# Attention scores of two heads side by side in the rows of the matrix engine, with three split products, in a decoder layer's kernel

## The chip, the cores and the metric

The kernel runs on one core of one Trainium2 chip. Its time is the device time of one execution, in microseconds (us). The median of three runs of the kernel before is 627.21 us (626.58 to 627.97). One further execution was taken by the hardware profiler; all rows of the profile are from it.

## The reference

A decoder layer on x of 512 tokens by 1024 channels in float32, cut here to what bears on the change:

```python
proj = h @ w_in[l]
q, k, v, p, g = jnp.split(proj, [512, 1024, 1536, 2048], axis=-1)
y_attn = moba_attention(q, k, v, rel_bias) @ w_branch_attn      # 8 heads x 64
y_pool = multiscale_pool(p, w_pool_group, pool_scale) @ w_branch_pool
gates  = sigmoid(g)                                             # two of 1024 channels
mixed  = gates[:, :, 0] * y_attn + gates[:, :, 1] * y_pool
h = layer_norm(ALPHA * h + mixed @ w_out, ln1_g, ln1_b)
a, u = jnp.split(h @ w_ffn_in, 2, axis=-1)
f = (gelu(causal_dwconv(a)) * u) @ w_ffn_out
h = layer_norm(ALPHA * h + f, ln2_g, ln2_b)
```

With 512 tokens and blocks of 256 the block-sparse attention picks every earlier block, so each head is causal softmax attention: the scores are q·k/8 plus a bias that depends on the distance and on the head.

## The kernel before, in words

**Precision.** Matrix products are made of float32 values split into a high part (fp32r) and what is left, the low part: `split` (L74-79) writes the high part with ScalarE (ACT, L76) and the low part with VectorE (DVE, L77). A product of two split operands then takes three matmuls of TensorE (PE): `mm3` (L245-251) gives high x high, low x high and high x low. Weights are fetched by DMA as raw float32 and split on the chip (`wraw`, `araw` to `whi`, `wlo`).

**Stages.** The v columns of the input projection come first, then the pool columns, then `seven(("i", n))` for n = 0 to 4: a projection of 256 columns of weights by seven quarter products in place of eight. n = 0 gives two groups of the pool branch; n = 1 to 4 give q and k of the pairs of heads 0 to 3 (pair p has the heads 2p and 2p+1, each with 64 channels). In rows of the trace the seven products have the names `sai`, `sbi`, `sci`; their sums go into `quad` tiles, half q and half k. The attention follows, and with it the matmuls of the two branches (`br`), so that PE has other work beside the softmax. Then come the gates, the output projection, the first layer norm, the feed-forward part and the second layer norm, which the change does not touch.

**Channels lie on partitions.** q and k of a pair are tiles of 128 partitions: the even head in 0 to 63, the odd one in 64 to 127. PE contracts over partitions.

**head(h)** (L442-459) prepares one head for its scores. Q1 gets the high part of q/8 in the head's own 64 partitions (ACT, L455) and the low part in the other 64 (DVE, L456). K1 gets the high part of -k in its own half (ACT, L452), KL the low part (DVE, L453). Two DMAs from SBUF to SBUF on SyncE's queue (SP, L459) copy those halves of K1 and KL into the other 64 partitions. `*behind` names instructions which these four wait for in the order of issue.

**scores(h)** (L545-573). For each block of 128 queries two matmuls over all 128 partitions: Q1 with K1, Q1 with KL. As both halves of K1 hold the same, these are (q high + q low) x k high and (q high + q low) x k low: four split products. They have 256, 256, 384 and 512 columns (only keys up to the block). DVE adds the bias strip and takes the row's maximum (L560), negates it (L563); ACT takes exp with that as its bias and sums it (L566); DVE inverts the sums (L568); GpSimd (POOL) multiplies (L571). Tiles `pp`, `nm`, `rs` are from the pool `aw`, with three buffers each. Bias strips are loaded two heads ahead, with three buffers.

**trans(h)** (L615-634) transposes P on PE by ten matmuls of 128 columns with the identity, and copies the result from PSUM to `PT`. **pv(p)** (L636-646) multiplies P with v for both heads of a pair; its matmuls fill 64 columns of the array each, the even head in the first 64 and the odd one in the others.

**The order around the change.** Each engine works through its own row of instructions in order. A scheduler in the build puts the instructions of the program into these rows; it may move an instruction ahead of others that wait, but `tc.keep_in_program_order(ins)` pins one, and `tc.issue_after(ins)` puts what stands inside it behind `ins`. PSUM has eight banks, dealt out in turn by `bank`. In the projection's loop (L576-606), `head(0)` stands behind n = 2, `head(1)` and `scores(0)` behind n = 3. Behind n = 4 come `scores(1)`, and the loop over the heads (L671-704): `head(h + 2)` behind the maximum and exps of head h; a gate's projection or a branch matmul; `scores(h + 2)`; for even h the PV of the pair before; `trans(h)`. At h = 5 four loads of x and two loads of gate weights (`fetch_raw`, into gX and gD) are issued behind the last use of `state["dup"]`, the copies between partitions.

## Time and profile before

| what | value |
|---|---|
| median of three runs | 627.21 us (626.58 to 627.97) |
| the profiled execution | 628.95 us |
| its span in the profile | 627.3 us |
| its granted clock of TensorE, mean | 0.998 |
| 70 to 90 us (end of the projection, first scores) | busy: PE 20.00, DVE 16.07, ACT 15.51 |
| 90 to 109.2 us (gates' first projections, scores of heads 2, 3) | busy: PE 19.20, DVE 15.71, ACT 12.68 |
| 109.2 to 154 us (scores 4 to 7, PV, transposes, branches) | busy: PE 44.60 of 44.80, DVE 33.11, ACT 25.86 |

How to read it: the span is the time from the first to the last recorded instruction of the profiled execution; the execution's own time is 1.65 us longer. Busy times are by engine: PE (TensorE's matmuls), PEld (its weight loads, which overlap them), DVE, ACT, POOL, SP. Matmuls are pipelined, so the ends of neighbours overlap; how long one keeps PE is read from start to start. `L556` is line 556 of the kernel before. In a row of the timeline, `x3` is a row of three alike, and `[0.48 <-DVE nm L563]` says that the engine stood idle for 0.48 us, and which instruction ended that. A clock of 1.00 is TensorE's full rate.

### The profile page before, as it was taken

The page shows a single profiled execution, that of the slowest core. Times are in us where ns is not written, and L with a number is a line of the kernel's source. Part 1 is how long each engine was busy: PE and PEld are TensorE (multiplying, and loading weights), DVE is VectorE, ACT ScalarE, POOL GpSimd, SP SyncE. Part 2 cuts the span into 40 slices and gives each one's busy share as a digit, 9 for nine tenths or more (in the row PEclk, how much of TensorE's full clock was granted, in tenths as well). Part 3 has the DMA queues.
Part 4 walks back from the last instruction along what each step waited for, and adds up shares of the span by engine and source line. Part 5 has one row for each costly group of instructions (what it writes and reads, how often), then busy time and mean ns, then how long its engine had stood idle before and what let it go on. Part 6 is the DMA issues. An engine that isn't in the chain of part 4 may idle for free.

```text
span 627.3 us, 10677 instructions
## 1 busy us (share of the span) xinstructions
PE 615.9 (98%) x4096; PEld 555.9 (89%) x4096; DVE 519.1 (83%) x801; ACT 360.1 (57%) x549; POOL 123.6 (20%) x133
## 2 busy tenths in 40 slices
PE   8999999999999999999998999999999999999995
PEld 6899998876899998889998999999999888888884
DVE  6978887885978988399987988899888869788886
ACT  6636777673756567134665666565656356555452
POOL 0033134353512101110110111011000302123201
PEclk9999999999999999999999999999999999999999
DMA  8477644339687425807557886877744996889805
GB/s 321 144 201 197 168 120 133 102 102 303 182 202 189 99 71 166 321 14 243 127 151 187 216 188 167 201 187 205 195 105 139 336 262 132 202 194 205 208 1 134
DMA packets 42322, 110.08 MB, mean 175 GB/s; under 512 B 4496, under 2 KB 5016, under 8 KB 42016
## 3 DMA queue, kind: packets, MB, share of 16 engines
q1 hardware_dynamic: 28224, 72.82, 34.7%
q0 software_dynamic: 13472, 35.67, 30.0%
q10 hardware_dynamic: 576, 0.92, 0.4%
q8 instruction: 32, 0.52, 0.4%
q14 instruction: 18, 0.15, 0.1%
HBM read 105.18 MB, written 3.17 MB: 173 GB/s over the span
## 4 chain that ended last, share of the span: by engine, by line
PE 94%; DVE 2%; DMA 2%; issue 0%; ACT 0%; POOL 0%; DVEq 0%; ACTq 0%; POOLq 0%
PE saf L247 5%; PE saf L251 5%; PE saf L250 5%; PE v L431 3%; PE fi L247 3%; PE fi L250 3%; PE fi L251 3%; PE wo L251 2%; PE wo L250 2%; PE wo L247 2%; PE sbf L247 2%; PE sbf L251 2%; PE sbf L250 2%; PE br L247 2%; PE br L250 2%; PE br L251 2%
## 5 line engine op out<-in xcount | busy, mean ns | idle before, releaser
L77 DVE TENSOR_TENSOR wlo<-araw,whi 128x1024 fp32r<-128x1024 f32 x58 | 71.6, 1242 | 5.8 <-ACT whi L76 5.1
L76 ACT ACTIVATE whi<-araw 128x1024 fp32r<-128x1024 f32 x58 | 60.7, 1057 | 21.8 <-PE saf L250 5.2
L77 DVE TENSOR_TENSOR wlo<-wraw,whi 128x1024 fp32r<-128x1024 f32 (+1 forms) x47 | 56.8, 1213 | 12.6 <-ACT whi L76 12.4
L76 ACT ACTIVATE whi<-wraw 128x1024 fp32r<-128x1024 f32 (+1 forms) x47 | 47.4, 1018 | 32.1 <-PE foa L251 4.2
L190 POOL DMA_DIRECT2D xraw<-in_w_fi x15 | 18.1, 1204 | 136.9 <-DVE fT L307 31.2
L76 ACT ACTIVATE whi<-tw 128x1024 fp32r<-128x1024 f32 (+1 forms) x30 | 29.5, 984 | 23.5 <-DMA tw<-in_w_fo 8.8
L247 PE MATMUL saf<-nT_hi,whi 128*128 128x256 f32 x136 | 38.1, 280 | 2.0 <-ACT fT L301 2.0
L77 DVE TENSOR_TENSOR wlo<-tw,whi 128x1024 fp32r<-128x1024 f32 (+1 forms) x30 | 33.4, 1128 | 6.4 <-ACT whi L76 6.4
L247 PE MATMUL saf<-hT_hi,whi 128*128 128x256 f32 x136 | 38.0, 279 | 0.1
L247 PE MATMUL sbf<-T_hi,whi 128*128 128x256 f32 x136 | 37.9, 279 | 0.0
L250 PE MATMUL saf<-hT_lo,whi 128*128 128x256 f32 x136 | 37.8, 278 | 0.0
L251 PE MATMUL saf<-nT_hi,wlo 128*128 128x256 f32 x136 | 37.8, 278 | 0.0
L251 PE MATMUL sbf<-T_hi,wlo 128*128 128x256 f32 x136 | 37.8, 278 | 0.0
L250 PE MATMUL saf<-nT_lo,whi 128*128 128x256 f32 x136 | 37.7, 277 | 0.0
L250 PE MATMUL sbf<-T_lo,whi 128*128 128x256 f32 x136 | 37.7, 277 | 0.0
L251 PE MATMUL saf<-hT_hi,wlo 128*128 128x256 f32 x136 | 37.7, 278 | 0.0
L250 PE MATMUL fi<-hT_lo,whi 128*128 128x256 f32 (+1 forms) x112 | 36.2, 326 | 0.0
L251 PE MATMUL fi<-hT_hi,wlo 128*128 128x256 f32 (+1 forms) x112 | 36.2, 326 | 0.0
L247 PE MATMUL fi<-hT_hi,whi 128*128 128x256 f32 (+1 forms) x112 | 36.1, 327 | 0.0
L571 POOL TENSOR_SCALAR pp<-pp,rs 128x128 f32<-128x128 f32 (+3 forms) x32 | 24.0, 765 | 24.7 <-DVE rs L568 11.1
L235 POOL DMA_DIRECT2D tw<-in_w_fo x18 | 15.6, 904 | 62.6 <-DVE wlo L77 62.6
L247 PEld LDWEIGHTS saf<-nT_hi,whi 128*128 128x128 f32 x136 | 25.5, 188 | 2.4 <-ACT fT L301 2.2
(357 smaller groups left out, 2227.3 us busy)
## 6 DMA issues: line engine op xcount, KB each, us to landing
tw<-in_w_fo POOLq DMA_DIRECT2D x20, 512.0 KB, 7.3
araw<-in_w_fi SPq DMA_DIRECT2D x17, 512.0 KB, 3.5
xraw<-in_w_fi SPq DMA_DIRECT2D x15, 512.0 KB, 4.4
xraw<-in_w_fi POOLq DMA_DIRECT2D x15, 512.0 KB, 6.9
araw<-in_w_c SPq DMA_DIRECT2D x12, 512.0 KB, 4.3
wraw<-in_w_fi SPq DMA_DIRECT2D x10, 512.0 KB, 3.6
wraw<-in_w_fo SPq DMA_DIRECT2D x10, 512.0 KB, 5.6
tw<-in_w_fo SPq DMA_DIRECT2D x10, 512.0 KB, 6.9
```

The lines of the kernel that those rows point to most:

```text
L76: state["hi"] = nc.scalar.activation(hi, src, AF.Copy)
L77: state["lo"] = nc.vector.tensor_tensor(lo, src, hi.bitcast(F32), op=ALU.subtract)
L190: state["acc"] = nc.gpsimd.dma_start(v, bass.AP(tensor=a.tensor, offset=a.offset, ap=[[pst, pn], [u.offset + S - a.offset, 2], [est, S]]), ...
L235: nc.gpsimd.dma_start(raw, half(then[1:], sl), accum_op=ALU.add)
L247: ins = nc.tensor.matmul(out_, wh, ah, start=start, stop=False, **kw)
L250: nc.tensor.matmul(out_, wh, al, start=False, stop=False, **kw)
L251: nc.tensor.matmul(out_, wl, ah, start=False, stop=stop, **kw)
L431: ins = nc.tensor.matmul(bs[j], xs_[j][a], (wh, wl)[b], start=kt == 0 and n == 0, stop=False)
L571: state["norm"] = nc.gpsimd.tensor_scalar(pp[:, offs[i]:offs[i] + n], pp[:, offs[i]:offs[i] + n], rs[:, i:i + 1], 1.0, op0=ALU.mult, op1=A ...
```

## The change

`head(h)` goes. `split_heads(p)` splits q and k of a whole pair with four instructions over all 128 partitions: `kh`, `qh` on ACT, `kl`, `ql` on DVE, one buffer each. Nothing is copied between partitions. `scores(p)` makes the scores of both heads of a pair: for each block of queries three products (high x high, high x low, low x high) by matmuls over 64 partitions, the even head's from partitions 0 to 63 and the odd head's from 64 to 127, in turns, and pinned to the order of the program. The product low x low is no longer formed. The softmax stands in a function of its own, called for one head after the other. `split_heads(0)` stands where `head(0)` stood; `split_heads(1)` stands behind `scores(0)` and is held behind the negated maximum and the exps of head 1; later pairs are split behind the transposes of an even head. Scores of a pair are issued at even h, ahead of the gate's projection. Strips and `aw` get four buffers for three. The order of the two heads within PV turns round, and the loads at h = 5 lose their second hold. The diff, cut to its core:

```diff
-        strips[h] = av.tile([P, S], F32, tag="strip", name=f"strip{h}")
+        strips[h] = av.tile([P, S], F32, tag="strip", name=f"strip{h}", bufs=4)
...
-    def head(h, *behind):
...
+    def split_heads(p, *behind):
+        qh, ql, kh, kl = QK[p] = [av.tile([P, S], F32R, tag=t, name=f"{t}_{p}", bufs=1)
+                                  for t in ("qh", "ql", "kh", "kl")]
         with ExitStack() as held:
             for ins in behind:
                 held.enter_context(tc.issue_after(ins.ins))
...
+            for hi, lo, raw, scale in ((kh, kl, raw_k[p], -1.0), (flip(qh), flip(ql), raw_q[p], DH ** -0.5)):
+                nc.scalar.activation(hi, raw, AF.Copy, scale=scale)
+                nc.vector.scalar_tensor_tensor(lo, raw, scale, hi.bitcast(F32), op0=ALU.mult, op1=ALU.subtract)
...
-    def scores(h):
+    def scores(p):
+        two = (2 * p, 2 * p + 1)
+        dst = {}
+        for h in two:
+            if h + 2 < H:
+                load_strip(h + 2)
+            b01 = bank(f"sc{h}_01")
+            dst[h] = [b01[:, :2 * P], b01[:, 2 * P:], bank(f"sc{h}_2")[:, :3 * P], bank(f"sc{h}_3")]
+        qh, ql, kh, kl = QK[p]
+        for i in range(NT):
+            n = max(2, i + 1) * P
+            q = slice(i * P, (i + 1) * P)
+            for m, (a, b) in enumerate(((qh, kh), (qh, kl), (ql, kh))):
+                for e, h in enumerate(two):
+                    own = slice(e * DH, (e + 1) * DH)
+                    ins = nc.tensor.matmul(dst[h][i], a[own, q], b[own, :n], start=m == 0, stop=m == 2)
+                    if e or m or i:
+                        tc.keep_in_program_order(ins)
+        for h in two:
+            softmax(h, dst[h])
...
-            nc.tensor.matmul(dst[i], Q1[h][:, q], K1[h][:, :n], start=True, stop=False)
-            nc.tensor.matmul(dst[i], Q1[h][:, q], KL[h][:, :n], start=False, stop=True)
...
-            head(0, state["add"], state["copy"])
+            split_heads(0, state["add"], state["copy"])
         elif n == 3:
...
-            head(1, state["add"], state["copy"])
...
-            aw = attn.enter_context(tc.tile_pool(name="aw", bufs=3, side="right", reuse_waits="tile"))
+            aw = attn.enter_context(tc.tile_pool(name="aw", bufs=4, side="right", reuse_waits="tile"))
             scores(0)
...
-            for e in range(2):
+            for e in (1, 0):
...
-        n = min(h + 1, H - 1)
-        with tc.issue_after(nms[n].ins), tc.issue_after(exps[n].ins):
+        n = min(h + 3 - h % 2, H - 1)
+        with ExitStack() as held:
+            for ins in (nms[n], exps[n], *copies.get(h - 2, ())):
+                held.enter_context(tc.issue_after(ins.ins))
             weights(limit)
...
-    scores(1)
     with tc.issue_after(exps[0].ins):
         flush()
+    split_heads(1, nms[1], exps[1])
     for h in range(H):
-        if h + 2 < H:
-            head(h + 2, nms[h], exps[h])
+        pair, late = divmod(h, 2)
+        if not late and h + 2 < H:
+            scores(pair + 1)
...
-        if h + 2 < H:
-            scores(h + 2)
...
+        if not late and h + 4 < H:
+            split_heads(pair + 2, nms[h + 3], exps[h + 3])
...
-            with tc.issue_after(state["norm"].ins), tc.issue_after(state["dup"].ins):
+            with tc.issue_after(state["norm"].ins):
```

What this does to the rows of the engines is shown at three places. First ACT at the first exps, before. `pp0` and `rs0` are P and its sums for head 0, `whi26` the high part of the 26th tile of weights, `k1_2`, `q1_2` the parts of head 2, `quad` and `sai`, `sbi` the sums and products of the projection:

```order
L566 ACTIVATE pp0_943,rs0_945<-pp0_943,nm0_944 128x256
L566 ACTIVATE pp0_943,rs0_945<-pp0_943,nm0_944 128x384
L566 ACTIVATE pp0_943,rs0_945<-pp0_943,nm0_944 128x512
L452 ACTIVATE k1_2_1144<-quad1_83 64x512
L76 ACTIVATE whi25_975<-araw4_721 128x1024
L455 ACTIVATE q1_2_1143<-quad1_83 64x4x128
L76 ACTIVATE whi26_1019<-wraw26_1018 128x1024
L299 ACTIVATE quad3_85<-sbi4_1004 128x256
L76 ACTIVATE whi27_1038<-wraw27_1037 128x1024
L537 ACTIVATE quad2_84<-sai3_810 128x512
L301 ACTIVATE quad3_85<-sai4_971 128x256
```

After, from the last exp of head 0 on:

```order
L567 ACTIVATE pp0_965,rs0_967<-pp0_965,nm0_966 128x512
L567 ACTIVATE pp1_982,rs1_984<-pp1_982,nm1_983 128x128
L567 ACTIVATE pp1_982,rs1_984<-pp1_982,nm1_983 128x256
L567 ACTIVATE pp1_982,rs1_984<-pp1_982,nm1_983 128x384
L567 ACTIVATE pp1_982,rs1_984<-pp1_982,nm1_983 128x512
L76 ACTIVATE whi26_1047<-wraw26_1046 128x1024
L446 ACTIVATE kh_1_1143<-quad1_83 128x512
L76 ACTIVATE whi27_1066<-wraw27_1065 128x1024
L525 ACTIVATE quad2_84<-sai3_809 128x512
L446 ACTIVATE qh_1_1141<-quad1_83 128x4x128
L299 ACTIVATE quad3_85<-sbi4_1032 128x256
L301 ACTIVATE quad3_85<-sai4_999 128x256
```

The exps of head 1 now stand directly behind those of head 0, and the high parts of pair 1 (`kh_1`, `qh_1`) behind them and two splits of weights. The two copies of the projection's last tile (L299, L301) stand behind `qh_1`.

PE at the same place of the program, where the projection's first product of tile 4 (`sai4`) ends; before, a gate's matmuls (`g0`) and then the D product (`sbi4`, of `iT4` with `whi24`):

```order
L251 MATMUL sai4_971<-inT2_hi_102,wlo25_976 128x256
L247 MATMUL sai4_971<-inT2_hi_102,whi25_975 128x256
L250 MATMUL sai4_971<-inT2_lo_103,whi25_975 128x256
L251 MATMUL sai4_971<-inT2_hi_102,wlo25_976 128x256
L247 MATMUL g0_1152<-xT_hi_73,whi26_1019 128x512
L250 MATMUL g0_1152<-xT_lo_74,whi26_1019 128x512
L247 MATMUL sbi4_1004<-iT4_hi_104,whi24_878 128x256
L250 MATMUL sbi4_1004<-iT4_lo_105,whi24_878 128x256
L251 MATMUL sbi4_1004<-iT4_hi_104,wlo24_879 128x256
```

After:

```order
L251 MATMUL sai4_999<-inT2_hi_102,wlo25_1004 128x256
L247 MATMUL sai4_999<-inT2_hi_102,whi25_1003 128x256
L250 MATMUL sai4_999<-inT2_lo_103,whi25_1003 128x256
L251 MATMUL sai4_999<-inT2_hi_102,wlo25_1004 128x256
L549 MATMUL sc2_01_1151<-kh_1_1143,qh_1_1141 128x256
L549 MATMUL sc3_01_1156<-kh_1_1143,qh_1_1141 128x256
L549 MATMUL sc2_01_1151<-kl_1_1144,qh_1_1141 128x256
L549 MATMUL sc3_01_1156<-kl_1_1144,qh_1_1141 128x256
L247 MATMUL sbi4_1032<-iT4_hi_104,whi24_877 128x256
L250 MATMUL sbi4_1032<-iT4_lo_105,whi24_877 128x256
```

Between `sai4` and `sbi4` there now stand four score matmuls of the heads 2 and 3, which need `kh_1`, `qh_1` and `kl_1`.

SyncE's queue of loads near the program's start, before (`wraw`, `araw`, `xr` are raw weights in the order of their use):

```order
L376 DMA wg_94<-in_w_group 128x512
L160 DMA wraw4_298<-in_w_c 128x1024
L160 DMA wraw5_309<-in_w_c 128x1024
L180 DMA araw0_315<-in_w_c 128x1024
L188 DMA xr0_106<-in_w_c 128x2x512
```

After:

```order
L376 DMA wg_94<-in_w_group 128x512
L160 DMA wraw4_298<-in_w_c 128x1024
L188 DMA gX_86<-in_w_c 128x2x512
L182 DMA gD_87<-in_w_c 128x512
L160 DMA wraw5_309<-in_w_c 128x1024
L180 DMA araw0_315<-in_w_c 128x1024
L188 DMA xr0_106<-in_w_c 128x2x512
```

The two loads of gate weights, gX and gD, now stand ahead of `wraw5`.

## The prediction

> **What bounds the kernel now.** I read the page's busy times first, then its chain of the work that ended last (shares of the span by engine).

> ```profile
> PE 615.9 (98%) x4096; PEld 555.9 (89%) x4096; DVE 519.1 (83%) x801; ACT 360.1 (57%) x549; POOL 123.6 (20%) x133
> ...
> PE 94%; DVE 2%; DMA 2%; issue 0%; ACT 0%; POOL 0%; DVEq 0%; ACTq 0%; POOLq 0%
> ```

> TensorE (PE) is busy for 98% of the span, and 94% of the chain lies on it. A saving therefore counts if it shortens PE's own row of work, and a wait costs if PE stands still in it. DVE and ACT are in order, so what they have in front of an operand of PE is what can make PE stand. All that the change touches lies between 75 and 154 us; I read that stretch on PE's timeline (start, busy us, engine, line, operation, tile, shape, how many).

> ```profile
> 112.04 0.28 PE L556 MATMUL sc<-k,q 128*128 128x256 f32 x1
> ...
> 112.86 0.39 PE L556 MATMUL sc<-k,q 128*128 128x512 f32 x1
> 113.10 0.40 PE L557 MATMUL sc<-kl,q 128*128 128x512 f32 x1
> 113.42 2.37 PE L642 MATMUL ob<-PT,vv 128*64 128x512 f32 x16
> 115.73 1.31 PE L626 MATMUL tr<-ident,pp 128*128 128x128 f32 x10
> ```

> The distance between starts is what an instruction takes of PE, since ends overlap. One head's scores run from 112.04 to 113.10 and one more 512-column step (113.10 − 112.86 = 0.24, 0.23 in the long row of branch matmuls): 1.29 us for two products of 256, 256, 384 and 512 columns, that is 0.117, 0.117, 0.178 and 0.23, or 0.64 a product. PV takes 2.31 (113.42 to 115.73).

> **The scores.** Before: eight heads at 1.29 are 10.3 us. After: three products of 64 rows for each head. If the matmuls of the two heads, which stand in different halves of the rows, run side by side, a pair of heads costs 3 × 0.64 = 1.92, four pairs 7.7, and 0.23 more where the order of the change leaves one 512-column matmul of head 0 alone: 7.95. **−2.35.** No row of before shows two matmuls in two halves of the rows. The nearest is PV, whose two heads stand in two halves of the columns. Here is PE's timeline cut to the 10 ns after PV's start:

> ```profile
> 113.42 0.65 PE L642 MATMUL ob<-PT,vv 128*64 128x512 f32 x2
> ```

> Two PV matmuls start within 10 ns, so these do run side by side. Bounds for the scores: −2.35 (as PV) and +5.3 (in turn: 24 × 0.64 = 15.3, plus 0.23). I take PV's way.

> **Changing the tiling.** PV also shows what it costs to go to another tiling and back. Three pieces of the last PV, on PE:

> ```profile
> 145.37 1.07 PE L642 MATMUL ob<-PT,vv 128*64 128x512 f32 x2
> 146.38 0.50 PE L247 MATMUL br<-zT_hi,whi 128*128 128x512 f32 x1
> 146.71 0.39 PE L250 MATMUL br<-zT_lo,whi 128*128 128x512 f32 x1
> ...
> 150.69 1.07 PE L642 MATMUL ob<-PT,vv 128*64 128x512 f32 x4
> 151.69 0.49 PE L247 MATMUL br<-oT_hi,whi 128*128 128x512 f32 x1
> 152.11 1.51 PE L642 MATMUL ob<-PT,vv 128*64 128x384 f32 x10
> 153.55 0.50 PE L250 MATMUL br<-oT_lo,whi 128*128 128x512 f32 x1
> ```

> The last full matmul ahead of PV keeps PE 0.32 (113.10 to 113.42) and the first behind it 0.33 (146.38 to 146.71), where 0.23 is usual; the first full one is also busy 0.50 instead of 0.39. So about 0.1 at each start and 0.1 at each end is drain, and as much again can be the first weight load, which has nothing to lie beside. Such a load is longer for the scores than for PV (columns: engine, operation, count, duration in ns least, median and most):

> ```profile
> L556 PEld LDWEIGHTS sc<-k,q x32: 187/188/192, 75.4 to 133.9; 128*128 128x128 f32 x32
> ```

> I take 0.20 at either end, 0.40 for a run of scores; the bounds are 0 and 0.1 + 0.188 twice, 0.58. By the order of the instructions the scores of after stand in 8 runs, so 8 × 0.40 = 3.2. Two of them follow transposes or PV, where one side is paid already (−0.2); PV stands in one run fewer (−0.35), transposes in two fewer (−0.2). **+2.45**, bounds −0.75 and +3.9.

> **The last PV.** It stands in three pieces before: 1.01 + 1.00 + 1.44 = 3.45 against 2.31 for the same 16 in one row, since the heads of a piece don't run paired. In the order of after it stands in two pieces, each with both heads: **−1.1**; bounds 0 (if its copies of P are again late) and −1.14.

> **Waits that go.** PE in the scores of head 1, and in the transposes of head 7:

> ```profile
> 86.23 0.69 PE L556 MATMUL sc<-k,q 128*128 128x256 f32 x3
> 86.88 0.39 PE L247 MATMUL sai<-inT_hi,whi 128*128 128x256 f32 x1
> 87.10 0.28 PE L250 MATMUL sai<-inT_lo,whi 128*128 128x256 f32 x1
> ...
> 87.45 0.69 PE L557 MATMUL sc<-kl,q 128*128 128x256 f32 x3
> 88.14 0.38 PE L251 MATMUL sai<-inT_hi,wlo 128*128 128x256 f32 x1
> 88.36 0.28 PE L247 MATMUL sai<-inT_hi,whi 128*128 128x256 f32 x1
> ...
> 141.70 0.55 PE L626 MATMUL tr<-ident,pp 128*128 128x128 f32 x3 [0.20 <-POOL pp L571]
> ```

> From 86.23 to 88.36 stand eight score matmuls and three of the projection: 1.29 + 3 × 0.117 = 1.64 of 2.13, so 0.5 is lost. After, no such lone pieces wait there, since head 1's scores are issued with head 0's. Head 7's transposes wait 0.20 for P; after, head 7's softmax comes with head 6's, long before. **−0.7**, bounds 0 and −0.9.

> **The new wait.** This is the largest term. After, the first scores of pair 1 stand in PE's row 60 matmuls behind the last scores of pair 0. They need the split of pair 1's q and k on ACT, and the code holds that split behind the last exp of head 1. On ACT, the table load, eight exps, two splits of weights and a copy stand ahead of it. PE's next rows, the projection's D product, need a copy that stands on ACT right behind the split, so PE has nothing it may do meanwhile. ACT and DVE in this stretch of before:

> ```profile
> 81.76 1.28 ACT L566 ACT_TABLE_LOAD   x1 [0.48 <-DVE nm L563]
> 83.05 0.40 ACT L566 ACTIVATE pp<-pp,nm 128x128 f32<-128x128 f32 x1
> ...
> 85.25 0.62 ACT L452 ACTIVATE k<-quad 64x512 fp32r<-64x512 f32 x1
> 85.78 1.05 ACT L76 ACTIVATE whi<-araw 128x1024 fp32r<-128x1024 f32 x1
> 86.72 0.61 ACT L455 ACTIVATE q<-quad 64x512 fp32r<-64x512 f32 x1
> ```

> ```profile
> 80.78 0.68 DVE L560 CUSTOM_DVE_ANT_0 pp<-sc,strip 128x512 f32<-128x512 f32 x1
> 81.51 0.17 DVE L563 TENSOR_SCALAR nm<-nm 128x4 f32<-128x4 f32 x1
> 82.51 0.42 DVE L307 TENSOR_TENSOR quad<-quad,sai 128x256 f32<-128x256 f32 x1 [0.83 <-PE sai L251]
> ...
> 83.42 0.69 DVE L453 SCALAR_TENSOR_TENSOR kl<-quad,k 64x512 fp32r<-64x512 f32 x1
> ...
> 86.86 1.23 DVE L77 TENSOR_TENSOR wlo<-araw,whi 128x1024 fp32r<-128x1024 f32 x1 [0.21 <-ACT whi L76]
> ```

> The chain begins when the projection's third product (sai3) leaves PE and DVE may add it. In the order of after there follow on DVE the two additions (82.51 to 83.42: 0.91), the 512-column maximum of head 0 (0.68), a split's low half (1.23), the maximum of head 1 (0.68) and the negation up to the table load (81.51 to 81.76: 0.25): 3.75. Then on ACT the table load (1.29), two heads' exps (2 × 2.20, from 83.05 to 85.25), a weight split (85.78 to 86.72: 0.94), k's high half (0.53), a second weight split (0.94), a copy of 512 columns (0.58, my estimate between k's step of 0.53 and its busy 0.62), and q's high half (0.62, to its end): 9.30. In all 13.05. In the same time PE has five 512-column score matmuls (0.7, paired), one change of tiling (0.4) and 60 matmuls of 256 columns (60 × 0.115 = 6.9): 8.0. PE stands for 13.05 − 8.0: **+5.05.** The table load is in the chain because exp is the first of its kind there. The halves have 128 partitions where k's row has 64; the time goes by the 512 columns. Bounds: if the two weight splits and the copy overlap better than here, −0.5; if DVE's low half waits for its high half, +0.5: 4.5 to 5.6.

> **Costed at nothing.** The four copies of a pair between partitions leave SP's queue; nothing on PE waited for them beyond the waits counted above. The splits are half as many instructions (four for a pair, not eight) and lie on ACT and DVE, which are not the bound outside of the wait above. Two loads for the gates, 768 KB, lose a hold and now stand at the start of SP's row, ahead of a weight load. Their cover is the lull of the DMA engines at 22 us (busy of PE, PEld, DVE, ACT and POOL, clock, DMA share, GB/s):

> ```profile
> 22.00:24.00 2.00, 2.00 (x10) 1.65 (x10) 2.00 (x3) 0.48 (x1) 0.00 (x0) 1.00 0.09 29
> ```

> There the DMA engines are 9% busy, so the weights behind come a little later and still in time. Without that cover, at the rate that this row gives for full engines (29 / 0.09 = 320 GB/s), 768 KB would be 2.4 us. Pairs 2 and 3 are split behind the exps of the pair before them; by the durations above pair 3's scores come at most 0.3 late, which the range holds.

> **The sum.** −2.35 + 2.45 − 1.1 − 0.7 + 5.05 = +3.35. The profiled run took 628.95 with a span of 627.3, so 632.3 for a run like it. That run lies 1.74 above the median of the runs (627.21); from the median the forecast is **630.5**, and the same work gives 629.5 to 631.5 with the wait at 4.5 to 5.6 and a part of the spread of the tiling's price.

> **Rivals.** (a) *The clock falls in the new wait.* PE's last matmul starts before 620; the windows behind it (same columns) and, from another place, PE behind an idle of 2.04 us and PE at the program's start:

> ```profile
> 620.00:624.00 4.00, 0.00 (x0) 0.00 (x0) 3.79 (x12) 0.29 (x1) 0.54 (x1) 1.00 0.74 225
> 624.00:627.30 3.30, 0.00 (x0) 0.00 (x0) 0.46 (x2) 0.00 (x0) 0.00 (x0) 0.56 0.34 116
> ```

> ```profile
> 334.57 0.39 PE L247 MATMUL saf<-nT_hi,whi 128*128 128x256 f32 x1 [2.04 <-ACT fT L301]
> ```

> ```profile
> 5.41 1.82 PE L431 MATMUL v<-whi,xT_hi 128*128 128x512 f32 x3
> 7.07 0.85 PE L431 MATMUL v<-whi,xT_lo 128*128 128x512 f32 x3
> ```

> After 4 us without a matmul the clock is still 1.00, and in the next 3.3 it is 0.56 on average: at half speed from about 624.4, some 4.5 us after the last matmul. After 2.04 it holds: that matmul is busy 0.39, no more than others behind a gap. The wait of 5.05 lies just past 4.5. At the program's start three 512-column matmuls take 1.66 instead of 0.69; a fall would cost that 1.0 and about as much again until the clock is back: +2, **632.5**. [...]

> (b) *Weight loads of the two halves come in turn.* A 256-column matmul with its own load takes 0.117, so two loads may need up to 0.23 where a pair has 0.117, and 0.23 where a 384-column pair has 0.178: (2 × 0.115 + 0.05) × 12 = +3.4, **633.9**. For it: 0.188 for a load is already longer than the matmul's step. Against it: PV's pairs. [...] If (b′) the matmuls themselves come in turn, so that the change doesn't do what it says, it is +7.7: **638.2**.

> (c) *Not slower: changing to half rows is free.* If PE drains only for halves of the columns, as in PV, the runs of scores cost nothing, 3.0 of the term for the tiling goes (8 × 0.40 less the 0.2) and +0.35 is left: **627.5**, no change. It decides from the price of a run: at 0.12 and less (8 × 0.28 = 2.2 under the forecast) the time falls below 628.46. Against it: PV's drain and reload at both ends.

> (d) *The wait is covered.* If exp's table is loaded earlier, or PE's row has something else that may go, the wait goes whole: 630.5 − 5.05, **625.5** and faster. Against it: ACT is in order, and the table load has nothing before it in the order that would call it.

> **How the numbers follow.** Forecast 0.50 (629.5 to 631.5); (a) 0.22; (b) and (b′) 0.10; (c) 0.10; (d) 0.08. A measurement of this kernel tells some 0.2%, 1.25 us, from no change: 625.96 to 628.46 is the same. So (d) is faster, 0.08; (c) and a part of the forecast's low edge the same, 0.12; all else slower, 0.80. The range takes in (c), (a), (b): 627.4 to 634.0, and leaves out (d) and (b′).

> **What would show it.** Right: PE idle about 5 us ahead of pair 1's first scores, released by the split's high half on ACT; score runs with two starts within 10 ns and 1.9 us a pair; 0.3 to 0.4 between starts at the ends of a run; the last PV in two pieces. Wrong: no such idle (then faster), clock under 1.00 after it (a), starts of a pair 0.1 apart (b), or 0.23 and more (b′).

## The result and the profile after

| kernel | median (runs) | ratio to before |
|---|---|---|
| before, beside the changed kernel | 627.59 us (626.58 to 628.11, 4 runs) | |
| changed | 635.43 us (632.73 to 636.72, 4 runs) | 1.0121, 95% interval 1.0081 to 1.0161 |
| changed, again, against 17 runs of before at 626.51 | 634.37 us (633.03 to 635.14, 4 runs) | 1.0119, 1.0099 to 1.0138 |

The change makes the kernel 7.8 to 7.9 us slower, where 3.3 were forecast, and its runs spread over 4 us. The profiled execution took 632.73 with a span of 631.0; it is the fastest of the four. Here is the changed kernel's page, busy times and the chain that ended last:

```profile
PE 616.8 (98%) x4128; PEld 555.0 (88%) x4128; DVE 508.2 (81%) x793; ACT 354.9 (56%) x541; POOL 125.1 (20%) x133
...
PE 77%; DVE 4%; ACT 2%; DMA 2%; issue 1%; DVEq 0%; ACTq 0%
```

PE is as busy as before, in more time. PE's share of the chain falls from 94% to 77%, DVE's rises from 2 to 4% and ACT's from 0 to 2% (the shares of this row add up to 86%, so part of the chain has no name in it). The place is the one that the prediction names. PE's timeline at the end of the projection's product `sai4` (after):

```profile
89.68 0.28 PE L251 MATMUL sai<-inT_hi,wlo 128*128 128x256 f32 x1
94.83 0.58 PE L549 MATMUL sc<-kh,qh 64*128 64x256 f32 x2 [4.87 <-ACT qh L446]
95.21 0.42 PE L549 MATMUL sc<-kl,qh 64*128 64x256 f32 x2
95.56 0.58 PE L247 MATMUL sbi<-iT_hi,whi 128*128 128x256 f32 x1
95.94 0.41 PE L250 MATMUL sbi<-iT_lo,whi 128*128 128x256 f32 x1
...
98.07 0.37 PE L251 MATMUL sbi<-iT_hi,wlo 128*128 128x256 f32 x1
98.28 0.28 PE L247 MATMUL sai<-inT_hi,whi 128*128 128x256 f32 x1
```

From 89.68 to 94.83 are 5.15 us, less the usual step of 0.115: PE loses 5.03, ended by q's high half on ACT. Behind the wait, matmuls of 256 columns are 0.21 apart instead of 0.115 until 98.28. The chain on ACT (after):

```profile
85.60 1.28 ACT L567 ACT_TABLE_LOAD   x1 [0.76 <-DVE nm L564]
86.90 0.40 ACT L567 ACTIVATE pp<-pp,nm 128x128 f32<-128x128 f32 x1
...
91.27 1.04 ACT L76 ACTIVATE whi<-wraw 128x1024 fp32r<-128x1024 f32 x1
92.22 0.61 ACT L446 ACTIVATE kh<-quad 128x512 fp32r<-128x512 f32 x1
...
93.69 0.57 ACT L525 ACTIVATE quad<-sai 128x512 f32<-128x512 f32 x1
94.16 0.62 ACT L446 ACTIVATE qh<-quad 128x512 fp32r<-128x512 f32 x1
```

It is the forecast chain: table load at 85.60, eight exps from 86.90 to 91.27, then the weight split, k, weights, the copy, q, whose end at 94.78 lets PE go. A run is a row of half-row score matmuls with other work on either side. One run of half-row scores (after):

```profile
78.62 0.28 PE L251 MATMUL sbi<-iT_hi,wlo 128*128 128x256 f32 x1
78.83 0.39 PE L549 MATMUL sc<-kh,ql 64*128 64x256 f32 x2
79.05 0.28 PE L549 MATMUL sc<-kh,qh 64*128 64x256 f32 x2
...
79.93 0.39 PE L549 MATMUL sc<-kh,qh 64*128 64x512 f32 x1
80.25 0.39 PE L247 MATMUL sai<-inT_hi,whi 128*128 128x256 f32 x1
80.48 0.28 PE L250 MATMUL sai<-inT_lo,whi 128*128 128x256 f32 x1
```

`x2` is a matmul of each head, begun together: a pair of 256 columns keeps PE 0.12. The four steps at the ends are 0.21 (78.62 to 78.83), 0.22, 0.32 and 0.23 where 0.115, 0.117, 0.23 and 0.115 are usual: 0.40 for the run, as taken.

**The profile of before was late by 2.7 us.** A second profile of the same kernel (before_again: median 626.15, 10 runs, ratio 1.0001) has a span of 624.5. What PE waited for, before's first profile (first line, in us, times, longest) and its second:

```profile
PE saf L247 <- ACT fT L301: 2.0, 1, 2.0
```

```profile
PE v L427 <- DMA wraw<-in_w_v: 0.4, 1, 0.4
PE tr L626 <- POOL pp L571: 0.2, 1, 0.2
```

The wait of 2.0 near 332 us is chance: feed-forward weights landed late in one execution (ACT stood 5.6 us for a load of `in_w_fi` ahead of it), and the whole 2.7 lies there. Since the forecast went from the median, it carries no error from that, but spans are compared with 624.5 below. To compare profiles without chance at the start and near 335 us, I take the time from the first pool projection to the first gate product (`sag`), the stretch with the attention in it. Before (second profile) and after:

```profile
27.41 0.39 PE L247 MATMUL p<-xT_hi,whi 128*128 128x512 f32 x1
...
171.10 0.28 PE L247 MATMUL sag<-xT_hi,whi 128*128 128x256 f32 x1
```

```profile
27.19 0.39 PE L247 MATMUL p<-xT_hi,whi 128*128 128x512 f32 x1
...
176.86 0.28 PE L247 MATMUL sag<-xT_hi,whi 128*128 128x256 f32 x1
```

143.69 and 149.67: +6.0. This "attention stretch" is given for every run below.

### The profile page after: what moved, and what is told of

The parts are those of the page before. It is cut to its first block, busy times and chain, and to the rows that moved or that the text cites. A ratio compares the mean times of both kernels' runs of the same rounds, so it can differ in the third digit from the quotient of the medians.

```text
span 631.0 us, 10674 instructions
## 1 busy us (share of the span) xinstructions
PE 616.8 (98%) x4128; PEld 555.0 (88%) x4128; DVE 508.2 (81%) x793; ACT 354.9 (56%) x541; POOL 125.1 (20%) x133
## 4 chain that ended last, share of the span: by engine, by line
PE 77%; DVE 4%; ACT 2%; DMA 2%; issue 1%; DVEq 0%; ACTq 0%
PE saf L247 4%; PE saf L251 4%; PE saf L250 4%; PE fi L247 3%; PE fi L251 3%; PE fi L250 3%; PE wo L251 2%; PE wo L250 2%; PE wo L247 2%; PE sbf L251 2%; PE sbf L247 2%; PE sbf L250 2%; PE sag L247 2%; PE sag L250 2%; PE sag L251 2%; PE br L247 2%
## 5 line engine op out<-in xcount | busy, mean ns | idle before, releaser
L77 DVE TENSOR_TENSOR wlo<-araw,whi 128x1024 fp32r<-128x1024 f32 x58 | 70.6, 1224 | 7.4 <-ACT whi L76 6.8
L76 ACT ACTIVATE whi<-araw 128x1024 fp32r<-128x1024 f32 x58 | 60.7, 1057 | 24.6 <-PE sag L250 5.1
L77 DVE TENSOR_TENSOR wlo<-wraw,whi 128x1024 fp32r<-128x1024 f32 (+1 forms) x47 | 55.6, 1187 | 16.0 <-ACT whi L76 15.9
L76 ACT ACTIVATE whi<-wraw 128x1024 fp32r<-128x1024 f32 (+1 forms) x47 | 47.6, 1018 | 36.8 <-DMA wraw<-in_w_fo 9.1
L76 ACT ACTIVATE whi<-tw 128x1024 fp32r<-128x1024 f32 (+1 forms) x30 | 29.5, 984 | 24.2 <-DMA tw<-in_w_fo 9.7
L77 DVE TENSOR_TENSOR wlo<-tw,whi 128x1024 fp32r<-128x1024 f32 (+1 forms) x30 | 33.4, 1128 | 7.4 <-ACT whi L76 7.4
L247 PE MATMUL saf<-hT_hi,whi 128*128 128x256 f32 x136 | 38.0, 280 | 0.1
L247 PE MATMUL saf<-nT_hi,whi 128*128 128x256 f32 x136 | 38.0, 279 | 0.1
L251 PE MATMUL sbf<-T_hi,wlo 128*128 128x256 f32 x136 | 37.9, 279 | 0.0
L251 PE MATMUL saf<-nT_hi,wlo 128*128 128x256 f32 x136 | 37.8, 278 | 0.0
L250 PE MATMUL saf<-nT_lo,whi 128*128 128x256 f32 x136 | 37.8, 278 | 0.0
L247 PE MATMUL sbf<-T_hi,whi 128*128 128x256 f32 x136 | 37.8, 278 | 0.0
L250 PE MATMUL saf<-hT_lo,whi 128*128 128x256 f32 x136 | 37.7, 278 | 0.0
L250 PE MATMUL sbf<-T_lo,whi 128*128 128x256 f32 x136 | 37.7, 277 | 0.0
L251 PE MATMUL saf<-hT_hi,wlo 128*128 128x256 f32 x136 | 37.7, 278 | 0.0
L250 PE MATMUL fi<-hT_lo,whi 128*128 128x256 f32 (+1 forms) x112 | 36.2, 326 | 0.0
L251 PE MATMUL fi<-hT_hi,wlo 128*128 128x256 f32 (+1 forms) x112 | 36.2, 326 | 0.0
L247 PE MATMUL fi<-hT_hi,whi 128*128 128x256 f32 (+1 forms) x112 | 36.1, 327 | 0.0
L247 PEld LDWEIGHTS saf<-nT_hi,whi 128*128 128x128 f32 x136 | 25.5, 188 | 0.5 <-ACT fT L301 0.3
```

Source lines behind the costliest of these rows:

```text
L76: state["hi"] = nc.scalar.activation(hi, src, AF.Copy)
L77: state["lo"] = nc.vector.tensor_tensor(lo, src, hi.bitcast(F32), op=ALU.subtract)
L247: ins = nc.tensor.matmul(out_, wh, ah, start=start, stop=False, **kw)
L250: nc.tensor.matmul(out_, wh, al, start=False, stop=False, **kw)
L251: nc.tensor.matmul(out_, wl, ah, start=False, stop=stop, **kw)
```

## The experiments

**The changed kernel again**, unchanged: three more profiles (after_again, and later after_p3 and after_p4).

> The changed kernel once more, unchanged, for its spread and a second profile. Theory A (the time is lost in PE's wait ahead of pair 1's first scores and in the half clock behind it): median 633 to 637, 1.009 to 1.016 of before, a wait of 4.8 to 5.2 us ended by the high half of q, and matmuls behind it at half rate; runs differ by how long the half rate lasts and by whether the wait of 2.0 us near 332 us of before comes back. Rival B (the loss sits behind the attention, in late transfers): the same wait, but most of the loss in idle time of PE after 160 us.

> The changed kernel, a third profile: the wait ahead of pair 1's scores 4.8 to 5.2 us again, and a span of 631 to 635. Theory A says that what differs between profiles is the time at half rate behind that wait (one stretch of some 3.4 us, or two) and the late loads (ahead of the last PV, near 335 us), and nothing else.

> The changed kernel, a fourth profile, with the expectations of the third: a wait of 4.8 to 5.2 us, a span of 631 to 635, and differences only in the time at half rate and in the late loads.

| profile | span | attention stretch, against 143.69 | wait ahead of the last PV | PE against 624.5's, from the `sag` on |
|---|---|---|---|---|
| after | 631.0 | +6.0 | 0.3 | +0.7 |
| after_again | 632.3 | +6.25 | 0.5 | +1.7 |
| after_p3 | 631.2 | +7.4 | 0.6 | +0.1 |
| after_p4 | 634.6 | +7.7 | 1.3 | +0.9 |

The wait is 4.8 to 4.9 us in all four. What differs is what theory A names, and one thing more: the moment at which TensorE's clock first rises to full rate after the program's start, 4.49 us in after_p3, 6.09 in after and 9.39 in after_p4. PE reaches the first pool product at 26.50, 27.19 and 28.93: about half a us later for each us (2.43 for 4.90).

The trace gives each change of the clock, with its time. In each of the 17 profiles of this case, all changes stand whole multiples of 3.413 us behind the first rise (to 0.01 us), wherever PE's waits lie; in after they stand at 94.84, 98.25 and 627.32 us, 26.00, 27.00 and 182.00 multiples behind the rise at 6.09. So in these profiles the changes lie on a grid of 3.413 us, and a window is a stretch between two of its points. Here are windows of after and then of after_p4 (from and to, length, busy of PE, PEld, DVE, ACT and POOL, the clock, DMA share, GB/s):

```profile
91.43:94.84 3.41, 0.01 (x2) 0.01 (x2) 2.64 (x4) 3.41 (x6) 3.40 (x5) 1.00 0.08 14
94.84:98.25 3.41, 3.41 (x16) 3.19 (x17) 1.38 (x2) 0.47 (x2) 1.85 (x1) 0.50 0.83 273
98.25:101.66 3.41, 3.41 (x35) 2.87 (x33) 2.60 (x7) 3.15 (x5) 0.00 (x0) 1.00 0.07 25
```

```profile
91.32:94.73 3.41, 0.40 (x4) 0.20 (x2) 0.84 (x2) 3.41 (x9) 3.40 (x7) 1.00 0.00 0
94.73:98.14 3.41, 1.59 (x8) 1.36 (x9) 3.21 (x4) 2.30 (x5) 3.41 (x2) 0.50 0.46 154
98.14:101.55 3.41, 3.41 (x18) 3.41 (x18) 0.80 (x2) 1.47 (x2) 0.28 (x1) 0.50 0.50 159
101.55:104.96 3.41, 3.41 (x33) 2.86 (x33) 3.38 (x14) 1.67 (x4) 0.00 (x0) 1.00 0.44 145
```

Here a window that is idle for the most part (PE is busy 0.01, 0.40 and 1.59 us of 3.41) is followed by half rate, and one that PE fills by full rate. In after the wait ends with a window, and one window runs at half; in after_p4 it ends in the middle of one, and two do. A wait of 4.85 us leaves at least 2.4 us of idle time in one window, wherever it falls. In all ten executions of the changed kernel on record the mean granted clock is 0.990 to 0.994, in those of the kernel before 0.996 to 0.998.

Half clock costs matmuls 1.4 us in after (94.83 to 98.28 is 3.45 for two pairs and twelve matmuls, 1.62, and one run, 0.40), 1.4 in after_again, 2.75 in after_p3 and 2.1 in after_p4 by the same sum. The mean of the four spans is 7.8 us over 624.5, the difference of the medians 7.9. Rival B, a loss behind the attention, falls: 6.0 to 7.7 of it lie in the stretch.

**Without the hold** (nohold):

```diff
-    split_heads(1, nms[1], exps[1])
+    split_heads(1)
```

> split_heads(1) without its hold behind head 1's maximum and exps, so that pair 1's q and k are split ahead of the first exp. Theory A: the wait (5.0) and the half clock behind it (1.4 or more) go, and one run of half-row scores is saved (0.4): median 626 to 628, 0.998 to 1.001 of before, with a spread of about 1.5 us. Rival B: 631 or more remains, as late transfers are untouched. Rival C (half-row scores cost more than 0.4 a run): 629 to 631.

629.63 us (626.87 to 631.74, 12 runs), ratio 1.0043 (1.0025 to 1.0061): 4.7 us under the changed kernel, but 1.6 above the top of what theory A expected. By the time alone it lies where rival C (a run costs more than 0.40) put it; the trace decides against C, since the ends of the runs cost 0.38 to 0.42 here too. In the profile the wait on q is gone, the clock stays at 1.00, and the attention stretch is +3.1. Two waits have come in its place (what PE waited for, nohold):

```profile
PE ob L642 <- ACT PT L628: 2.2, 1, 2.2
...
PE sc L549 <- ACT quad L525: 0.9, 1, 0.9
```

By what ended them, the scores of pair 1 now wait for what DVE (another 0.3) and ACT have still to read in PSUM, and the last PV waits for copies of P. And the clock does fall in some executions: five of the twelve have a mean granted clock of 0.994 or 0.995 (median 631.10 us), the other seven 0.996 to 0.998 (median 627.65, within what theory A expected). So the long wait was the hold's doing, and with the hold gone shorter ones show that had been hidden behind it.

**Work in the wait** (warm): in `scores(1)`, ahead of its first matmul,

```diff
+        if p == 1:
+            for _ in range(20):
+                nc.tensor.matmul(dst[2][3], xT_hi[:, 0, :P], xT_hi[:, 0, :], start=True, stop=True)
```

> The wait is left as it is, but 20 matmuls of 512 columns, whose result is overwritten, stand in PE's row ahead of pair 1's first scores (4.55 us of work with operands that are there). Theory A: PE is busy in the wait, the clock stays at 1.00, and only the half-rate part goes: 1.4 to 3 us under the changed kernel, median 631 to 633, spread under 2 us. Rival D (the clock has no part in it; the matmuls after the wait are slow for want of weights or data): no gain, 634 to 637.

632.61 us (631.07 to 635.06, 6 runs), ratio 1.0100 (1.0078 to 1.0122): 1.8 under the changed kernel. The runs spread over 4.0 us, twice what was expected, and the interval of the ratio overlaps the changed kernel's (1.0099 to 1.0138), so the size is not sharp. In its profile PE waits 0.3 for q, the clock is 1.00 from 80 us on, and the first matmuls behind the scores are at full rate; in all six executions the mean granted clock is 0.996 to 0.998, as before the change. So the matmuls behind the wait are slow because the clock falls in it, and rival D falls; the gain fits theory A's 1.4 to 3 us.

**The table of exp ahead of time** (pretable, pretable16, pretable_w): behind the split of pair 0 one exp of a column,

```diff
+            with tc.issue_after(state["copy"].ins):
+                nc.scalar.activation(OUT, eps_t, AF.Exp)
```

with OUT a new tile of one column, a new tile of 16, or a column of the tile `warm`, which is there and no longer used.

> An exp of one column early on ACT, so that the table for exp is loaded ahead of the attention. Theory A: the table load (1.29) leaves the chain, the wait is 3.5 to 3.9 us; if the clock falls only after some 4.5 us without matmuls, as at the end of the program, it stays at 1.00 and the time is 630 to 632; if a window of 3.4 us that runs freely decides, some runs still fall and the median is 631 to 634 with a wide spread.

> The early exp of one column again, its result in a tile of 16 columns where it had one: nothing but the place of later tiles in SBUF differs from the run before. Theory F (the slow growth of all matmul steps in that run came from tiles that were moved by 4 bytes): steps of 256 columns are 0.115 us again, and the time is 631 to 633: the changed kernel less 1.3 for the table load, less 1.4 if the clock stays at 1.00 in a wait of 3.5 us. Rival (the early exp itself does it): 639 again.

> The early exp of one column a third time, its result written into a tile that is there and no longer used, so that no tile moves in SBUF. Theory F (moved tiles made all matmul steps slower from the program's start): steps of 256 columns are 0.115 us and nothing grows from 5 us on; the wait is 3.5 us; with the clock still falling in it, as it did at 3.5 us in the run before, 632 to 635. Rival (the early exp or what its table does is to blame): 637 or more again.

639.78 (1.0207), 637.59 (1.0186) and 632.10 us (631.36 to 632.52, 5 runs; ratio 1.0091, 1.0073 to 1.0108). The first two were misses: the wait is 3.5 as expected, yet every stage from 5 us on is slower, by 7 us and more in sum. Theory F holds in the third, where no tile moves. Its profile shows how the clock falls in a shorter wait, PE's timeline and two windows:

```profile
93.72 0.39 PE L549 MATMUL sc<-kh,qh 64*128 64x256 f32 x2 [3.56 <-ACT qh L446]
```

```profile
91.64:95.05 3.41, 1.33 (x11) 1.20 (x12) 3.41 (x4) 2.56 (x6) 3.41 (x2) 1.00 0.47 147
95.05:98.46 3.41, 3.41 (x18) 3.41 (x17) 1.61 (x3) 2.23 (x4) 0.53 (x1) 0.50 0.53 166
```

PE is back at 93.72 and works at full rate for 1.3 us; only at the window's end, 95.05, the clock halves, for 3.4 us. So the 4.5 us of the program's end are no threshold: here the clock halved behind a window with 1.33 us of work and 2.08 us of idle time in it.

**The order of heads in PV, on the kernel before** (b_ord):

```diff
-            for e in range(2):
+            for e in (1, 0):
```

> The kernel before with one edit of the change alone: the order of the two heads within PV. The last PV then stands in two pieces with both heads instead of three. By the prediction's term: 1.1 us less, with one change of tiling fewer up to 1.4: median 0.9978 to 0.9985 of before. If the pairing is not what made the pieces long: no change.

626.03 us (11 runs), ratio 0.9996 (0.9987 to 1.0005): no gain. PE and ACT in its profile:

```profile
146.68 1.08 PE L642 MATMUL ob<-PT,vv 128*64 128x512 f32 x4 [0.90 <-ACT PT L628]
```

```profile
145.08 1.06 ACT L76 ACTIVATE whi<-wraw 128x1024 fp32r<-128x1024 f32 x1 [2.04 <-DMA wraw<-in_w_br]
146.04 0.58 ACT L628 ACTIVATE PT<-tr 128x512 f32<-128x512 f32 x1
```

The last PV is in two pieces, as wanted, and now waits 0.9 for P: on ACT its copy stands behind a split of branch weights that are still on their way. That is what the expectations call theory E.

**The loads at h = 5 one head later** (nohold_late, on nohold):

```diff
-        if h == 5:
-            with tc.issue_after(state["norm"].ins):
+        if h == 6:
+            with tc.issue_after(state["norm"].ins), tc.issue_after(copies[5][1].ins):
```

> The version without the hold, and in it the four loads of x and the gate loads of h = 5 one head later, behind head 5's copies of P, so that they start behind the last branch weights. Theory E (PE's wait ahead of the last PV comes from branch weights that land late beside these loads; ACT splits them in front of the copies of P): the wait of 2.2 us in the profile goes, median 626.5 to 628 with a spread of about 2 us, against 629.6 without this edit. Rival (the weights are late for another reason, or the loads now make the gates wait): 629 to 631, and the wait stays or moves behind 165 us.

629.35 us (627.94 to 630.98, 6 runs), ratio 1.0056 (1.0044 to 1.0068): no gain that can be told. The wait ahead of the last PV is 1.2 in its profile instead of 2.2, but the clock fell at another place. PE in pair 1's scores:

```profile
91.33 0.46 PE L549 MATMUL sc<-kh,qh 64*128 64x512 f32 x1 [0.29 <-DVE nm L561]
92.74 0.50 PE L549 MATMUL sc<-kh,qh 64*128 64x512 f32 x1 [0.95 <-ACT quad L525]
```

Two idles of 0.3 and 0.95 us, 1.4 us apart, and from 94.11 the matmuls behind them are 0.43 apart until 97.5: half clock again. In nohold's profile the same idles left it at 1.00. Here are the windows with the idles in them, nohold_late's with the next one, then nohold's:

```profile
90.70:94.11 3.41, 2.17 (x12) 1.12 (x11) 2.56 (x14) 3.41 (x10) 3.38 (x8) 1.00 0.06 18
94.11:97.52 3.41, 3.41 (x10) 2.64 (x9) 2.32 (x7) 1.27 (x6) 2.54 (x3) 0.50 0.44 141
```

```profile
89.38:92.79 3.41, 2.17 (x22) 1.44 (x21) 1.53 (x11) 3.41 (x12) 2.31 (x5) 1.00 0.37 130
92.79:96.20 3.41, 3.41 (x16) 2.55 (x17) 3.41 (x10) 1.43 (x3) 3.07 (x5) 1.00 0.09 20
```

PE is busy 2.17 us in both, with 12 matmuls in one and 22 in the other, since the windows begin at different places of the program. What of this work counts for the clock, no run shows. Whether the loads or chance shortened the PV wait stays open.

**Late weights behind the copies of P** (nohold_fix, b_ord_fix, after_fix): the last branch weights, which PE needs some 60 matmuls behind the last PV, are held behind head 7's copies.

```diff
-            for ins in (nms[n], exps[n], *copies.get(h - 2, ())):
+            for ins in (nms[n], exps[n], *copies.get(h if h == H - 1 else h - 2, ())):
```

(b_ord_fix: the same hold, for h = 7 alone, in b_ord.)

> The version without the hold, and in it the last branch weights are held behind head 7's copies of P, so that on ACT no split of late weights stands ahead of these copies. Theory E (the wait ahead of the last PV comes from weights that land late and block ACT's row): the wait goes and the median is 627 to 628 against 629.6 without it, less spread. Rival (the weights are needed there at once): the wait moves to the branch matmuls behind the last PV and the time stays at 629 to 630.

> The kernel before with the order of heads in PV turned round, and the last branch weights held behind head 7's copies of P. Theory E (the gain of the paired last PV was there, but PE then waited for the copies of P that stand behind a split of late weights): the wait of 0.9 us goes and the 1.1 to 1.4 show: 0.9975 to 0.9985 of before. Rival (the pieces cost nothing that can be saved): 1.000.

> The changed kernel with one edit: the last branch weights held behind head 7's copies of P. Theory E alone: its wait of 0.3 to 0.5 us ahead of the last PV goes, and what it is longer in other runs; median 633 to 634, 0.5 to 1.5 under the changed kernel. Rival: no difference, 634 to 636.

nohold_fix: 627.71 us (12 runs), ratio 1.0021 (1.0008 to 1.0035); no wait ahead of the last PV, though in the profile the clock fell as in nohold_late, behind the same two idles. b_ord_fix: 625.47 us (625.03 to 626.40, 12 runs), ratio 0.9984 (0.9971 to 0.9996), attention stretch −0.8, and a wait of 0.4 ahead of the last PV in place of 0.9: **the one version that beats both kernels**, by about 0.8 us. The hold alone was not tried on the kernel before. after_fix: 634.69 us (633.31 to 635.94, 4 runs), ratio 1.0146 (1.0129 to 1.0163): no gain, a miss, though its profile has no wait ahead of the last PV. Its half clock lasts two windows (2.85 by the sum above), and a gain of half a us can't be told in that spread.

**Pair 1's scores behind the first gate** (s_swap_fix, on nohold_fix): `scores(1)` is called behind `in_tile` at h = 0 and held behind its last matmul, and in every pair the product with q's low half comes first.

```diff
-            for m, (a, b) in enumerate(((qh, kh), (qh, kl), (ql, kh))):
+            for m, (a, b) in enumerate(((ql, kh), (qh, kl), (qh, kh))):
...
-        if not late and h + 2 < H:
+        if h and not late and h + 2 < H:
             scores(pair + 1)
...
             in_tile(*fill.pop(0))
+            if h == 0:
+                scores(1)
```

> The version before this one, and in it pair 1's scores are held behind the first gate's matmuls, and the product with q's low half comes first, so that a run of scores starts when all four halves are there. Theory A with the price of 0.4 a run: no wait on PSUM banks in pair 1's scores (1.6 us in the profile of the version without the hold), one run of scores fewer than the changed kernel, a wait of up to 1.8 us for the first gate's weights: 625.5 to 628. If short waits there still make the clock fall: 628 to 630.

627.36 us (626.23 to 629.09, 12 runs), ratio 1.0017 (1.0005 to 1.0029), attention stretch +0.9, the clock at 1.00. PE waits 0.2 and 0.6 for the gate's weights and 0.5 for q's low half. This version is 1.1 us behind the kernel before and 1.9 behind b_ord_fix, which has the same order in PV and the same hold. Their attention stretches differ by 1.6; with the waits of both taken off, 0.8 is left, which is the scores with their changes of tiling.

## Why the prediction was wrong

Right in sign and place; wrong in size, and the measured median lies above its range (634.0). Term by term, the changed kernel's first profile against before:

| term | forecast | measured in the profile |
|---|---|---|
| scores, three products in halves | −2.35 | −1.9 |
| changing the tiling | +2.45 | +2.7 |
| last PV | −1.1 | −1.0, and a new wait ahead of it, +0.4 |
| waits that go | −0.7 | −0.7 |
| the new wait | +5.05 | +5.03 |
| half clock behind it | 0 (rival a: +2) | +1.4 |
| sum | +3.35 | +5.9 (attention stretch +6.0) |

- **The scores.** The two heads run side by side, as taken from PV; rivals (b) and (b′) fall, since pairs start together and step by 0.12 to 0.23. Weight loads of 64 rows take 0.19, as those of 128 rows did, and begin in pairs as well. The eight runs take 8.4 us without their ends where 7.95 were forecast. The 0.45 is pair 3's run, which takes 2.55 us where pair 2's takes 2.14, alike in all four profiles. q's low half is late there (DVE and PEld, after):

```profile
128.27 0.99 DVE L447 SCALAR_TENSOR_TENSOR ql<-quad,qh 128x512 fp32r<-128x512 f32 x1
```

```profile
129.31 0.19 PEld L549 LDWEIGHTS sc<-kh,ql 64*128 64x128 f32 x2 [0.16 <-DVE ql L447]
```

Behind that the two heads fall out of step up to the run's end; why they do, no run shows. The prediction allowed pair 3 "at most 0.3 late" and put it into no term.
- **Changing the tiling.** The price of a run, 0.40, is right (0.38 to 0.41 in the six runs at full clock whose ends can be read), and rival (c) falls: 3.2 for the 8 runs. Of this, 0.45 comes back at the transposes: the step out of them costs 0.11, at 9 places before and at 7 after, and at two of the seven it is at once the first step of a run of scores. That is the 0.2 and 0.2 of the forecast. The 0.35 for PV in one run fewer does not show here: the next row is taken from each row of PV matmuls to the instruction behind it and holds most of its ends, so that 1.45 were forecast for the two and 1.0 came. The run at half clock is not counted twice; its 0.4 stands in this term. That a run's price is made up of drain and a first weight load was an estimate; no run shows the parts.
- **The last PV.** The matmuls gained what was forecast, but the bound "0 if its copies of P are again late" was nearer the truth: b_ord shows no gain, b_ord_fix shows 0.8. The term looked at PE's pieces and not at what made them, a copy on ACT behind late weights. In the other profiles of the changed kernel this wait is 0.5 to 1.3.
- **The new wait.** The chain was right link by link: 13.05 less 8.0 were forecast; from 81.86, where the projection's sai3 leaves PE, to 94.83 are 12.97, of which PE works 7.94, and 5.03 are left. k's high half took 0.61 us on 128 partitions where it had taken 0.62 on 64.
- **The clock. This is the step that failed most.** The prediction read a time from the program's end (half clock some 4.5 us after the last matmul), set it against a wait of 5.05, gave the fall 0.22 and put nothing for it into the sum. The clock fell in every profile of the changed kernel, in waits of 3.5 us, and in two profiles behind two idles of 1.2 us together. In the windows of after, after_p4 and pretable_w shown above it fell behind 3.40, 3.01 and 2.08 us of idle time in one window of 3.41, and both readings of the prediction were of where the windows happened to lie: at the program's end the clock fell 4.5 us after the last matmul in before, but 1.97 us after it in after_p3, behind a window that still held 1.44 us of work; the 2.04 us in before lay across a window's end, 1.71 on one side and 0.33 on the other. The idle did not start the window either: in pretable_w the fall comes 1.3 us after PE was back. The forecast's case should have been (a), and with a price of 1.4 to 2.75 instead of 2 flat: 632 to 633.3.
- **The rest of the median.** The first profile was a good execution: its parts give 6 us, and the four profiles are 7.8 over before's on average, 4.4 more than forecast. On average over the four, half clock is 1.9 of that, late weights near 335 us 0.85 (0.1 to 1.7, against none in before's second profile), the wait ahead of the last PV 0.7, pair 3's scores 0.45, the tiling 0.25 and the PV itself 0.1. The weights are not explained: no run shows why they are later in the changed kernel.
- **Costed at nothing.** The loads for the gates at the program's start cost nothing: at 27 us PE stands where the first rise of the clock puts it, before the change and after (27.14 us with a rise at 5.80 in b_ord_fix, 27.19 with 6.09 in after). Fewer splits and no copies between partitions gave nothing either, as said.

By the first profile the change's idea saves 1.9 us of score matmuls and 0.7 of waits and pays 2.7 for changes of tiling: it gains nothing even without the wait, and s_swap_fix, 0.8 behind b_ord_fix without its waits, shows no better.

## What to carry to other kernels

Count the places at which the matrix engine changes its tiling before counting the products that are saved: here a run of half-row matmuls had to save over 0.4 us to be worth it, and only pair 2's did, a whole pair in one run (1.9 us and 0.4 for its ends, instead of 2.6). When a step is held behind others on an in-order engine, add up the whole row ahead of it, and set half clock behind a long idle into the sum, not into the rivals (here 1.4 to 2.75 us behind waits of 4.8 to 4.9, and a window of half rate behind one of 3.56 as well). A term that shortens work in front of a late operand is worth nothing until the operand comes earlier (the last PV: no gain in b_ord, 0.8 us in b_ord_fix): look at what the engine waits for once the term is gone.
